# A decoder trunk in float32 on one core: the MLP's first matrices as token-major column pairs with 7-product steps, and the residual kept in HBM

## The chip, the cores and the metric

The kernel runs on one core of one Trainium2 chip. A core has five engines with queues of their own: PE (TensorE, the matrix multiplier, whose weight loads the profile lists apart as PEld), DVE (VectorE), ACT (ScalarE), POOL (GpSimd) and SP (SyncE, which here only issues DMA transfers). PE writes its results into PSUM, eight banks of 128 x 512 float32. Everything else works in SBUF, and the weights come from HBM. The metric is the time of one execution on the device in microseconds (us); the time before is the median of three runs.

## The reference, cut to what matters

A residual stream x of 256 tokens by 2048 goes through two layers. The first is a retention layer, the second a multi-head latent attention layer, and each is followed by an MLP with 8192 hidden columns:

```python
def rms_norm(x, gain):
    xf = x.astype(jnp.float32)
    y = xf * lax.rsqrt(jnp.mean(xf * xf, axis=-1, keepdims=True) + RMS_EPS)
    return (y * gain.astype(jnp.float32)).astype(x.dtype)

def sq_relu_mlp(h, w1, w2):
    return jnp.square(jax.nn.relu(h @ w1)) @ w2

for layer in range(DEPTH):              # DEPTH = 2
    if layer < N_A_LAYERS:              # layer 0
        x = x + retention(rms_norm(x, norm_mix[layer]), ...)
    else:                               # layer 1
        ...                             # shared keys and values from x
        x = x + mla_attention(rms_norm(x, norm_mix[layer]), ...)
    x = x + sq_relu_mlp(rms_norm(x, norm_mlp[layer]), mlp_w1[layer], mlp_w2[layer])
```

`mlp_w1[layer]` is 2048 x 8192 and `mlp_w2[layer]` is 8192 x 2048, all in float32.

## The kernel before

**Products.** A float32 product is made of three products of a faster type: each operand is split into a high part (a rounded copy, made by ACT) and a low part (the rest, made by DVE), and PE adds high x high, high x low and low x high. `split` (lines 139 to 148) makes the two parts, of weights as of activations. So every weight that streams in costs one ACT cast and one DVE subtraction, in pieces of 128 x 1024, into the buffers `wh` and `wl` (five of each). The raw weights come in chunks of 1 MB into three `raw` buffers, one SP transfer each.

**Activations.** An `act` tile (line 73, 20 buffers) holds the two parts of 256 feature rows for all 256 tokens, feature-major, that is, with features on partitions. Other scratch tiles of 2 KB per partition come from `f2k` (14 buffers). The residual x stays in SBUF for the whole kernel as eight tiles of 128 tokens x 512 columns (line 111). PSUM has four `acc` banks, two `tp` banks and a pair of banks `at`.

**The MLP** (`mlp`, from line 650) goes through the hidden columns in four groups of 2048. In each group it first makes the hidden columns (up), then multiplies them by their rows of the second matrix (down).

- Up, in this kernel, is `gemm_t` (line 212): eight column tiles of 256 hidden columns, each over 16 feature tiles of 128 rows. The weights are the stationary operand, so the result comes out feature-major. The high weights multiply both parts of the activations in one matmul of 512 columns (line 231), the low weights only the high part, 256 columns (line 227). `up` (from line 656) adds the two halves of each bank, multiplies by the token's norm (a row over tokens, `row`, made by `token_row`, lines 393 to 405), applies ReLU and squares, and splits the result into a `hid` tile.
- Down is `gemm_pair` (line 288): two pairs of column blocks (1024 output columns each), each over eight row pairs of 256 hidden rows. Here the activations are stationary and the weights stream, so the result is token-major. One row pair is `quad` (line 239): a 2 x 2 block product (two token blocks, two row blocks, two column blocks). Five of the eight row pairs take the usual eight block products, 24 matmuls of 512 columns. The three row pairs named in `SEVEN` (line 32) take seven products instead, 21 matmuls, in the manner of Strassen and Winograd; for these, `quad` makes sums of the weight blocks on DVE (`u`, lines 270 to 276) and `up` makes sums of the activations' blocks (`hids`, lines 667 to 674). The accumulators c11, c12, c21 and c22 take the four `acc` banks, p1 and p5 the two `tp` banks, p6 and p7 the two banks of `at`.
- `pair_to_x` (line 322) ends a pair: twelve DVE additions from PSUM and SBUF into x, and two ACT copies.
- In the last group the second pair is computed as two plain blocks (`mlp_w2t`), so that the end of the layer isn't held up.

At a layer's border `into_next` (line 407) adds the block to x, sums its squares, and transposes the block on PE into `act` tiles for the next layer (`x_block_t`, line 365), scaled by the norm's gain. The norm of a token, a scalar, is applied afterwards.

**Order.** Work off the main line is put on a queue (`later`, line 81) that counts weight chunks: `later(2, turn)` emits `turn` two chunks later, and `need` runs the queue early when a step needs its results. That gives an order of urgency, not the order on the engines. A planner then places the instructions of each engine by its own costs, buffers and this urgency, and adds the semaphores; so on an engine an instruction written later can stand ahead of one written earlier. Once placed, each engine runs its instructions in that order.

In the attention, `score` makes the softmax of two heads on DVE and ACT, and its `turn` (lines 913 to 924) transposes the probabilities on PE (tile `ptp`), `later(2, ...)` after the scores.

Of the kernel before, what the change touches and what calls it, by code (L numbers as in the profile page):

```python
# [11 lines left out]
F32 = mybir.dt.float32  # L12
# [19 lines left out]
SEVEN = (1, 4, 7)  # L32
# [18 lines left out]
def yoco(ctx: ExitStack, tc: tile.TileContext, a):  # L51
# [59 lines left out]
    x = [[pool.tile([P, 512], F32, name=f"x_{t}_{b}") for b in range(NB)] for t in range(NT)]  # L111
# [176 lines left out]
    def gemm_pair(w, chunk0, act, kinds, name, done):  # L288
# [33 lines left out]
    def pair_to_x(c, b):  # L322

        for (t, j), key in (((0, 0), "c11"), ((0, 1), "c12"), ((1, 0), "c21"), ((1, 1), "c22")):
            nc.vector.tensor_tensor(x[t][b + j], c[key], x[t][b + j], op=ALU.add)
        p1, p5, v, u = (f2k([512], f"pair_{i}") for i in range(4))
        nc.scalar.copy(p1, c["p1"])
        nc.scalar.copy(p5, c["p5"])
        nc.vector.tensor_tensor(v, c["p6"], p1, op=ALU.add)
        nc.vector.tensor_tensor(u, c["p7"], v, op=ALU.add)  # L330
        nc.vector.tensor_tensor(x[0][b], x[0][b], p1, op=ALU.add)
        nc.vector.tensor_tensor(v, p5, v, op=ALU.subtract)
        nc.vector.tensor_tensor(p5, p5, u, op=ALU.subtract)
        nc.vector.tensor_tensor(x[0][b + 1], x[0][b + 1], v, op=ALU.add)
        nc.vector.tensor_tensor(x[1][b], x[1][b], u, op=ALU.add)
        nc.vector.tensor_tensor(x[1][b + 1], x[1][b + 1], p5, op=ALU.add)
# [28 lines left out]
    def x_block_t(b, g0s, outs, name):  # L365

        for k2 in range(2):
            tp = transposed(
                lambda t, j: x[t][b][:, (2 * k2 + j) * P : (2 * k2 + j + 1) * P], f"{name}_tp{b}{k2}"
            )  # L370
            for g0, out in zip(g0s, outs):
                v = act_tile(f"{name}{g0}_{b}{k2}")
                split_act(v, tp, [gain(g0 + b * 4 + k2 * 2 + j) for j in range(2)])
                out.append(v)
# [9 lines left out]
    def add_to_x(acc, b, ss, name):  # L384
        for t in range(NT):
            if acc is not None:
                nc.vector.tensor_tensor(x[t][b], acc[t], x[t][b], op=ALU.add)
            if ss is not None:
                square_sum(x[t][b], ss[t][:, b : b + 1], f"{name}_{t}{b}")

    row = pool.tile([P, S], F32, name="row")

    def token_row(r, row, name):

        wide = f2k([NT, P], f"{name}_wide")
        for t in range(NT):
            nc.vector.tensor_copy(wide[:, t], r[t].to_broadcast([P, P]))

        def turn():
            tp = bank("tp", [S], f"{name}_rtp")  # L400
            for t in range(NT):
                nc.tensor.transpose(tp[:, t * P : (t + 1) * P], wide[:, t], ident)
            nc.scalar.copy(row, tp)

        later(1, turn)

    def into_next(ss, g0s, outs, r, name, row=None):


        def done(b, acc):  # L410
            add_to_x(acc, b, ss, name)
            later(1, lambda: x_block_t(b, g0s, outs, name))
            if b == NB - 1:
                r.extend(x_rstd(ss, name))
                if row is not None:
                    token_row(r, row, name)

        return done
# [95 lines left out]

    def load_x(b):
        for t in range(NT):
            nc.sync.dma_start(x[t][b], a["x"][t * P : (t + 1) * P, b * 512 : (b + 1) * 512])
            square_sum(x[t][b], ss0[t][:, b : b + 1], f"n0_{t}{b}")
# [85 lines left out]
    for h in range(RH):  # L604
# [39 lines left out]
    act, r = [], []  # L644
    gemm_blocks(
        a["ret_w_out"], lambda b: b * 8, y_act, 32, "ro", into_next(ss, [G_MLP0], [act], r, "n1", row)
# [3 lines left out]
    def mlp(layer, act, row, done):  # L650
        w1, w2 = a[f"mlp_w1_{layer}"], a[f"mlp_w2_{layer}"]
        f0 = 0
        for gi, nf in enumerate(GROUPS):
            hid = []

            def up(acc, f):
                u = f2k([2, S], f"u{layer}_{f}")
                for i in range(2):
                    nc.scalar.copy(u[:, i], acc[i][:, S:])
                    nc.vector.tensor_tensor(u[:, i], acc[i][:, 0:S], u[:, i], op=ALU.add)  # L660
                both = row.unsqueeze(1).to_broadcast([P, 2, S])
                nc.vector.scalar_tensor_tensor(u, u, 0.0, both, op0=ALU.max, op1=ALU.mult)
                nc.scalar.activation(u, u, AF.Square)
                v = act_tile(f"hid{layer}_{f}")
                split_act(v, u)
                more = None
                if f - 2 * f0 in SEVEN:
                    blocks = u.rearrange("p j (t n) -> p (j t) n", t=NT)
                    sums = f2k([4, P], f"us{layer}_{f}")
                    nc.vector.tensor_tensor(sums[:, 0:2], blocks[:, 0:2], blocks[:, 1:4:2], op=ALU.subtract)  # L670
                    nc.vector.tensor_tensor(sums[:, 2], sums[:, 1], blocks[:, 0], op=ALU.subtract)
                    nc.vector.tensor_tensor(sums[:, 3], blocks[:, 2], sums[:, 2], op=ALU.add)
                    more = act_tile(f"hids{layer}_{f}")
                    split_act(more, sums.rearrange("p (j t) n -> p j (t n)", j=2))
                hid.append(v)
                both_hid.append((v, more))

            both_hid = []
            for f in range(2 * f0, 2 * (f0 + nf)):
                gemm_t(w1, f * 2, act, KD, f"u{layer}_{f}", lambda acc, f=f, f0=f0: up(acc, f))  # L680
            last = gi == len(GROUPS) - 1
            for p in range(2):
                if last and p:
                    for b in (2, 3):
                        gemm(
# [11 lines left out]
                gemm_pair(  # L697
                    w2, p * 32 + 2 * f0, both_hid, [i in SEVEN for i in range(2 * nf)], f"d{layer}_{gi}{p}", add
                )
# [4 lines left out]
    mlp(0, act, row, into_next(ss, [G_KV, G_MIX1], [act_kv, act_q], r2, "n2"))  # L704
# [170 lines left out]
    def score(b, qt, qpe):  # L875
# [48 lines left out]
        later(2, turn)  # L924
# [15 lines left out]
    gemm_blocks(a["mla_w_o"], lambda b: b * 4, o_act, KD, "wo", into_next(ss, [G_MLP1], [act], r, "n3", row))  # L940

    def finish(b, acc):
        if acc is not None:
            add_to_x(acc, b, None, "")
# [3 lines left out]
    mlp(1, act, row, finish)  # L948
# [90 lines left out]
```

## Time and profile before

| | |
|---|---|
| median of three runs | 2540.93 us (2538.68 to 2542.39) |
| the profiled execution's own time | 2538.38 us |
| its span, first to last instruction | 2536.5 us |
| mean granted TensorE clock | 1.000 |
| HBM read / written | 469.70 MB / 2.10 MB |
| POOL busy | 103.4 us |

The profile records every instruction with engine, start and duration. A group row names the line, the engine, the operation, the tile written, the tiles read, shapes and count; then come total busy time, mean duration in ns, and the engine's idle time just before these instructions with what ended it. In the timeline, rows give the start and the time from the first start to the last end of the instructions merged in the row. PE's matmuls are pipelined, so the records of neighbours overlap and what one costs is the distance between starts, not the duration.

### The profile page before, as it was taken

What the parts mean: (1) busy time and instruction counts of PE and PEld (TensorE: products, weight loads), DVE (VectorE), ACT (ScalarE), POOL (GpSimd) and SP (SyncE); (2) the same over time, 40 slices, a digit from 0 to 9 for tenths busy, and PEclk for the clock granted to TensorE, in tenths of its full rate; (3) what the DMA queues carried; (4) which work ended last, traced back from release to release, by engine and by line L of the source; (5) the groups of instructions that cost most, each with busy time, mean ns of one, the idle gap of its engine ahead of it and who ended that gap; (6) DMA issues with size and microseconds to landing.
All of it is one profiled execution on the core that took longest, in us unless ns stands there. A gap on an engine that the chain in (4) does not pass through costs nothing.

```text
span 2536.5 us, 32194 instructions
## 1 busy us (share of the span) xinstructions
PE 2516.8 (99%) x12710; PEld 2143.9 (85%) x12710; DVE 1758.4 (69%) x2336; ACT 1329.4 (52%) x1799; POOL 103.4 (4%) x131
## 2 busy tenths in 40 slices
PE   8999999999999999999999999999999999999999
PEld 7888888888888888888888888988888888888887
DVE  6655555554556786877877757877567868878775
ACT  6444444444445555555555656555555555555553
POOL 6200000000000000000000001100000000000000
PEclk9999999999999999999999999999999999999999
DMA  8555555545555465555555464433554554545544
GB/s 297 180 182 184 181 180 177 187 183 183 189 192 183 171 227 183 189 209 184 198 198 193 149 216 170 160 131 138 180 186 183 205 193 170 219 176 205 198 178 166
DMA packets 71575, 473.88 MB, mean 187 GB/s; under 512 B 8192, under 2 KB 9344, under 8 KB 18176
## 3 DMA queue, kind: packets, MB, share of 16 engines
q1 hardware_dynamic: 71280, 471.78, 51.2%
q8 instruction: 100, 1.64, 0.3%
q14 instruction: 51, 0.42, 0.0%
q10 hardware_dynamic: 144, 0.05, 0.0%
HBM read 469.70 MB, written 2.10 MB: 186 GB/s over the span
## 4 chain that ended last, share of the span: by engine, by line
PE 94%; DVE 2%; POOL 2%; DMA 0%; ACT 0%; issue 0%; SPq 0%; DVEq 0%; ACTq 0%; POOLq 0%
PE u_acc L231 19%; PE u_acc L227 10%; PE d_c L312 6%; PE d_c L313 6%; PE d_c L311 6%; PE ro_acc L205 2%; PE ro_acc L204 2%; PE ro_acc L203 2%; PE rv_acc L205 2%; PE rv_acc L203 2%; PE rv_acc L204 2%; PE rk_acc L231 2%; PE rq_acc L231 2%; PE rg_acc L205 2%; PE rg_acc L204 2%; PE rg_acc L203 2%
## 5 line engine op out<-in xcount | busy, mean ns | idle before, releaser
L231 PE MATMUL u_acc<-n,u_wh 128*128 128x512 f32 x2048 | 718.4, 398 | 0.0
L227 PE MATMUL u_acc<-n,u_wl 128*128 128x256 f32 x2048 | 564.8, 281 | 0.0
L231 PEld LDWEIGHTS u_acc<-n,u_wh 128*128 128x128 f32 x2048 | 381.1, 188 | 88.9
L143 DVE TENSOR_TENSOR u_wl<-u_raw,u_wh 128x1024 fp32r<-128x1024 f32 x256 | 311.4, 1222 | 155.2 <-ACT u_wh L142 154.2
L227 PEld LDWEIGHTS u_acc<-n,u_wl 128*128 128x128 f32 x2048 | 386.6, 189 | 5.6
L142 ACT CAST u_wh<-u_raw 128x1024 fp32r<-128x1024 f32 x256 | 267.9, 1051 | 201.5 <-PE u_acc L231 151.5
L142 ACT CAST d_wh<-d_raw 128x1024 fp32r<-128x1024 f32 (+1 forms) x256 | 247.0, 983 | 160.4 <-PE d_c L313 82.3
L143 DVE TENSOR_TENSOR d_wl<-d_raw,d_wh 128x1024 fp32r<-128x1024 f32 (+1 forms) x256 | 280.4, 1130 | 33.4 <-ACT d_wh L142 32.8
L312 PE MATMUL d_c<-d_wl,hid 128*128 128x512 f32 x644 | 251.3, 390 | 0.0
L313 PE MATMUL d_c<-d_wh,hid 128*128 128x512 f32 x644 | 250.6, 389 | 0.0
L311 PE MATMUL d_c<-d_wh,hid 128*128 128x512 f32 x644 | 246.7, 389 | 0.0
L143 DVE TENSOR_TENSOR d_wl<-d_u,d_wh 128x1024 fp32r<-128x1024 f32 x84 | 101.7, 1222 | 79.9 <-ACT d_wh L142 79.9
L142 ACT CAST d_wh<-d_u 128x1024 fp32r<-128x1024 f32 x84 | 87.6, 1049 | 122.8 <-PE d_c L313 108.2
L312 PEld LDWEIGHTS d_c<-d_wl,hid 128*128 128x128 f32 x644 | 120.8, 188 | 28.2 <-DVE d_wl L143 2.7
L311 PEld LDWEIGHTS d_c<-d_wh,hid 128*128 128x128 f32 x644 | 120.9, 188 | 24.8
L313 PEld LDWEIGHTS d_c<-d_wh,hid 128*128 128x128 f32 x644 | 120.9, 188 | 24.4
L143 DVE TENSOR_TENSOR ro_wl<-ro_raw,ro_wh 128x1024 fp32r<-128x1024 f32 x64 | 78.4, 1225 | 84.2 <-ACT ro_wh L142 84.2
L143 DVE TENSOR_TENSOR rg_wl<-rg_raw,rg_wh 128x1024 fp32r<-128x1024 f32 (+1 forms) x68 | 79.5, 1174 | 60.8 <-ACT rg_wh L142 60.8
L142 ACT CAST ro_wh<-ro_raw 128x1024 fp32r<-128x1024 f32 x64 | 67.4, 1053 | 94.5 <-PE ro_acc L205 86.5
L143 DVE TENSOR_TENSOR rv_wl<-rv_raw,rv_wh 128x1024 fp32r<-128x1024 f32 x64 | 79.2, 1248 | 41.4 <-ACT rv_wh L142 41.4
L203 PE MATMUL rg_acc<-rg_wh,a 128*128 128x512 f32 x256 | 101.2, 396 | 5.3 <-ACT a L145 5.3
L142 ACT CAST rg_wh<-rg_raw 128x1024 fp32r<-128x1024 f32 (+1 forms) x68 | 67.8, 998 | 72.4 <-PE rv_acc L205 46.7
(313 smaller groups left out, 5135.4 us busy)
## 6 DMA issues: line engine op xcount, KB each, us to landing
u_raw<-in_mlp_w SPq DMA_DIRECT2D x128, 1024.0 KB, 4.8
d_raw<-in_mlp_w SPq DMA_DIRECT2D x112, 1024.0 KB, 4.8
rv_raw<-in_ret_w_gv SPq DMA_DIRECT2D x32, 1024.0 KB, 4.8
ro_raw<-in_ret_w_out SPq DMA_DIRECT2D x32, 1024.0 KB, 4.8
rg_raw<-in_ret_w_gv SPq DMA_DIRECT2D x28, 1024.0 KB, 4.7
uq_raw<-in_mla_w_uq SPq DMA_DIRECT2D x24, 768.0 KB, 4.2
rq_raw<-in_ret_w_qk SPq DMA_DIRECT2D x16, 1024.0 KB, 4.8
rk_raw<-in_ret_w_qk SPq DMA_DIRECT2D x16, 1024.0 KB, 4.8
```

What stands on the lines that cost most here:

```text
L142: nc.scalar.copy(h, src)
L143: nc.vector.tensor_tensor(l, src, h.bitcast(F32), op=ALU.subtract)
L203: nc.tensor.matmul(acc[t], ah, rh, start=k == 0, stop=False)
L204: nc.tensor.matmul(acc[t], ah, rl, start=False, stop=False)
L205: nc.tensor.matmul(acc[t], al, rh, start=False, stop=k == nk - 1)
L227: nc.tensor.matmul(acc[f][:, 0:S], wl[:, cols], a[:, 0], start=False, stop=False)
L231: nc.tensor.matmul(acc[f], wh[:, cols], a.rearrange("p i s -> p (i s)"), start=k == 0, stop=k == nk - 1)
L311: nc.tensor.matmul(dst, ah, bh, start=n == 0, stop=False)
L312: nc.tensor.matmul(dst, ah, bl, start=False, stop=False)
L313: nc.tensor.matmul(dst, al, bh, start=False, stop=n == total[key] - 1)
```

## The change

Four things change together.

1. The first matrices of the MLP are stored in the same blocks as the second ones (`_quads`), and up uses `gemm_pair`: eight pairs of column blocks of 1024 hidden columns per layer, two per group, each over eight row pairs of 256 features. Three of the eight row pairs take seven products. So the layer's input, too, gets sums of its blocks for these row pairs (`with_sums`, called from `x_block_t`). The result is token-major: the token's norm is applied as a scale of ACT's Relu, and four hidden tiles per pair are transposed on PE, squared by ACT and split, with sums where needed. The token row goes.
2. The 7-product row pairs are numbers 3, 5 and 7 instead of 1, 4 and 7.
3. A pair ends in `pair_out`: six ACT copies out of PSUM, then eight DVE instructions, into `f2k` tiles. For up they are the hidden columns. For down they are added to the residual in HBM by accumulating DMA transfers that POOL issues, except in the last group of a layer, where they are added to x in SBUF. The residual lives in HBM (`x_home`) and is loaded into `act` tiles (`x_tiles`) before the retention's output matrix, before the last group's down matrices of each layer, and before the attention's output matrix; at each layer border it is stored again. The first load of x, for its squares, goes to scratch tiles. There are 24 `act` buffers instead of 20.
4. In the attention the transposes of the probabilities come `later(3)` instead of `later(2)`.

```diff
-SEVEN = (1, 4, 7)
+SEVEN = (3, 5, 7)
...
-        return pool.tile([P, 2, 2, S], dtype, tag="act", bufs=20, name=name)
+        return pool.tile([P, 2, 2, S], dtype, tag="act", bufs=24, name=name)
...
-    x = [[pool.tile([P, 512], F32, name=f"x_{t}_{b}") for b in range(NB)] for t in range(NT)]
+    dram = ctx.enter_context(tc.tile_pool(name="dr", bufs=1, space=bass.MemoryType.DRAM))
+    x_home = [[dram.tile([P, 512], F32, name=f"xh_{t}_{b}") for b in range(NB)] for t in range(NT)]
+    x = [[None] * NB for t in range(NT)]
+
+    def x_tiles(home, name):
+
+        for b in range(NB):
+            both = act_tile(f"x_{name}{b}", F32)
+            for t in range(NT):
+                x[t][b] = both[:, t].rearrange("p i s -> p (i s)")
+                nc.gpsimd.dma_start(x[t][b], home(t, b))
...
-                queue.append((clock[0] + 1, -1, lambda: done(made)))
+                queue.append((clock[0] + 1, -1, lambda: done(pair_out(made, name))))
...
+    def pair_out(c, name):
+
+        o = {}
+        for key in ("c22", "c12", "c11", "c21", "p1", "p5"):
+            o[key] = f2k([512], f"{name}_{key}")
+            nc.scalar.copy(o[key], c[key])
+        v, u = (f2k([512], f"{name}_{i}") for i in "vu")
+        nc.vector.tensor_tensor(v, c["p6"], o["p1"], op=ALU.add)
         nc.vector.tensor_tensor(u, c["p7"], v, op=ALU.add)
...
+        nc.vector.tensor_tensor(v, o["p5"], v, op=ALU.subtract)
+        nc.vector.tensor_tensor(o["p5"], o["p5"], u, op=ALU.subtract)
+        for key, add in (("c11", o["p1"]), ("c12", v), ("c21", u), ("c22", o["p5"])):
+            nc.vector.tensor_tensor(o[key], o[key], add, op=ALU.add)
+        return [[o["c11"], o["c12"]], [o["c21"], o["c22"]]]
+
+    def with_sums(blocks, name):
+
+        blocks = blocks.rearrange("p j (t n) -> p (j t) n", t=NT)
+        sums = f2k([4, P], f"{name}_sum")
+        nc.vector.tensor_tensor(sums[:, 0:2], blocks[:, 0:2], blocks[:, 1:4:2], op=ALU.subtract)
+        nc.vector.tensor_tensor(sums[:, 2], sums[:, 1], blocks[:, 0], op=ALU.subtract)
+        nc.vector.tensor_tensor(sums[:, 3], blocks[:, 2], sums[:, 2], op=ALU.add)
+        more = act_tile(f"{name}_more")
+        split_act(more, sums.rearrange("p (j t) n -> p j (t n)", j=2))
+        return more
...
+                elif 2 * b + k2 in SEVEN:
+                    u = f2k([2, S], f"{name}u_{b}{k2}")
+                    for j in range(2):
+                        nc.scalar.activation(u[:, j], tp[:, j], AF.Copy, scale=scales[j])
+                    split_act(v, u)
+                    out.append((v, with_sums(u, f"{name}{b}{k2}")))
...
             add_to_x(acc, b, ss, name)
-            later(1, lambda: x_block_t(b, g0s, outs, name))
+            blocks = [x[t][b] for t in range(NT)]
+            for t in range(NT):
+                nc.gpsimd.dma_start(x_home[t][b], blocks[t])
+            later(1, lambda: x_block_t(blocks, b, g0s, outs, name, sums))
...
+            def up(c, p, hid=hid, blocks=blocks):
+
+                need(r, NT)
+                for t in range(NT):
+                    for i in range(2):
+                        nc.scalar.activation(c[t][i], c[t][i], AF.Relu, scale=r[t])
+
+                def turn():
+                    for q in range(4):
+                        name = f"hid{layer}_{p}{q}"
+                        tp = transposed(
+                            lambda t, j: c[t][q // 2][:, (q % 2 * 2 + j) * P : (q % 2 * 2 + j + 1) * P], f"{name}_tp"
+                        )
+                        u = f2k([2, S], f"{name}_u")
+                        nc.scalar.activation(u, tp, AF.Square)
+                        v = act_tile(name)
+                        split_act(v, u)
+                        blocks.append((v, with_sums(u, name) if len(blocks) in SEVEN else None))
+                        hid.append(v)
+
+                later(1, turn)
+
+            for p in range(f0 // 2, (f0 + nf) // 2):
+                gemm_pair(
+                    w1, p * 8, act, [i in SEVEN for i in range(8)], f"u{layer}_{p}", lambda c, p=p, up=up: up(c, p)
+                )
+            if last:
+                x_tiles(lambda t, b: x_home[t][b], f"mlp{layer}")
...
-                    pair_to_x(c, 2 * p)
-                    if last:
-                        done(2 * p, None)
-                        done(2 * p + 1, None)
...
+                    for j in range(2):
+                        b = 2 * p + j
+                        if last:
+                            done(b, [c[t][j] for t in range(NT)])
+                            continue
+                        for t in range(NT):
+                            nc.gpsimd.dma_start(x_home[t][b], c[t][j], accum_op=ALU.add)
...
-        later(2, turn)
+        later(3, turn)
...
-        arrays[f"mlp_w1_{i}"] = _chunks(g["mlp_w1"][i], 256, 8)
+        arrays[f"mlp_w1_{i}"] = _quads(g["mlp_w1"][i])
```

More of the change, by code (lines that the diff above doesn't have):

```diff
@@ L653, in mlp @@
         for gi, nf in enumerate(GROUPS):
[L654 to L676, printed above, removed]
@@ L678, in mlp @@
-            both_hid = []
-            for f in range(2 * f0, 2 * (f0 + nf)):
-                gemm_t(w1, f * 2, act, KD, f"u{layer}_{f}", lambda acc, f=f, f0=f0: up(acc, f))
-            last = gi == len(GROUPS) - 1
+            hid, blocks = [], []
+            kinds = [i in SEVEN for i in range(2 * nf)]
+            last = gi == len(GROUPS) - 1
+            def up(c, p, hid=hid, blocks=blocks):
[16 more added lines that the diff above has]
+                later(1, turn)
@@ L684, in mlp @@
                     for b in (2, 3):
+                        need(hid, 2 * nf)
                         gemm(
```

70 lines of the change are left out of this document (25 added, 45 removed).

## The prediction

> **What bounds the kernel now.** I read the page first: the engines' busy time, then the chain that ended last, then the groups of instructions. From the page:
>
> ```profile
> span 2536.5 us, 32194 instructions
> PE 2516.8 (99%) x12710; PEld 2143.9 (85%) x12710; DVE 1758.4 (69%) x2336; ACT 1329.4 (52%) x1799; POOL 103.4 (4%) x131
> PE 94%; DVE 2%; POOL 2%; DMA 0%; ACT 0%; issue 0%; SPq 0%; DVEq 0%; ACTq 0%; POOLq 0%
> ```
>
> PE is busy nearly all the time and carries 94% of the chain, so a change is worth what it takes off PE's stream, less any new wait of PE. The view by windows, cut where the MLP of layer 0 passes from its first matrix (up) to its second (down) and back, gives the prices. The columns are the stretch, its length, then busy us of PE, PEld, DVE, ACT, POOL, the granted clock, the DMA share and GB/s:
>
> ```profile
> 750.40:841.70 91.30, 91.30 (x524) 79.40 (x523) 61.16 (x81) 50.17 (x72) 1.52 (x4) 1.00 0.51 185
> 841.70:924.90 83.20, 83.20 (x368) 68.53 (x367) 70.49 (x81) 46.91 (x53) 0.00 (x0) 1.00 0.50 189
> 924.90:1015.10 90.20, 90.20 (x514) 78.37 (x512) 65.33 (x82) 47.19 (x64) 0.00 (x0) 1.00 0.55 199
> 1015.10:1098.20 83.10, 83.10 (x367) 68.48 (x366) 70.39 (x81) 46.88 (x53) 0.00 (x0) 1.00 0.50 189
> ```
>
> PE has no gap in any of them and the granted clock is 1.00. An up stage of 8 column tiles takes 90.2 us (512 matmuls); a down stage of two column pairs takes 83.1 us (366 matmuls: per pair five row pairs of 24 and three of 21). The first stage is 1.1 us longer, since the transposes of the layer's input lie in it. DVE is the second busiest, 70.4 of 83.1 us in a down stage.
>
> **The up matrices as column pairs.** In the new kernel two up pairs replace one up stage. A column pair of the first matrix has 8 row pairs (2048 rows), three of them with 7 products: 183 matmuls of 128x512, just as a down pair. So I take the down stage's row for two of them: 83.1 us instead of 90.2, 7.1 us less in each of 8 stages (4 groups, 2 layers): **-57 us**. The down stages keep their count, since SEVEN still holds 3 of 8.
>
> **The transposes.** The output now lies token-major, so each up pair turns 4 hidden tiles with 4 transposes each: 16 x 16 = 256. A row of before's transposes (starts, durations):
>
> ```profile
> L162 PE MATMUL n_tp<-cst,x 128*128 128x128 f32 x96 | 12.6, 272 | 0.0
> 756.01 1.04 PE L162 MATMUL n_tp<-cst,x 128*128 128x128 f32 x8
> 756.80 0.36 PE L227 MATMUL u_acc<-n,u_wl 128*128 128x256 f32 x1
> 757.00 0.40 PE L231 MATMUL u_acc<-n,u_wh 128*128 128x512 f32 x1
> 757.24 0.28 PE L227 MATMUL u_acc<-n,u_wl 128*128 128x256 f32 x1
> 757.36 0.39 PE L231 MATMUL u_acc<-n,u_wh 128*128 128x512 f32 x1
> ```
>
> Each record lasts 272 ns, but they overlap: eight start at 756.01, and the matmul after the next starts at 757.00, where it normally follows its forerunner by 0.12 us (757.24 to 757.36). Eight therefore cost 757.00 - 0.12 - 756.01 = 0.87 us, 0.11 each: 256 x 0.11 = **+28 us**. [...]
>
> **DVE and ACT in an up pair.** Durations:
>
> ```profile
> L143 DVE TENSOR_TENSOR d_wl<-d_raw,d_wh 128x1024 fp32r<-128x1024 f32 x214 | 251.5, 1217 | 21.3 <-ACT d_wh L142 20.6
> L271 DVE TENSOR_TENSOR d_u<-d_raw 128x1024 f32<-128x1024 f32 x42 | 51.2, 1218 | 0.2
> L275 DVE TENSOR_TENSOR d_u<-d_u,d_raw 128x512 f32<-128x512 f32 x42 | 28.7, 684 | 0.3
> L143 DVE TENSOR_TENSOR hid<-u,hid 128x512 fp32r<-128x512 f32 x64 | 44.0, 687 | 5.7 <-ACT hid L142 5.7
> L670 DVE TENSOR_TENSOR us<-u 128x256 f32<-128x256 f32 x24 | 10.0, 417 | 0.0
> L672 DVE TENSOR_TENSOR us<-u,us 128x128 f32<-128x128 f32 x24 | 6.8, 283 | 0.0
> L663 ACT ACTIVATE u<-u 128x512 f32<-128x512 f32 x64 | 40.6, 634 | 14.5 <-DVE u L662 14.4
> L142 ACT CAST d_wh<-d_raw 128x1024 fp32r<-128x1024 f32 x214 | 221.9, 1053 | 109.6 <-PE d_c L313 45.7 <-PE u_acc L231 16.6 <-PE d_acc L205 14.3
> L328 ACT COPY pair<-d_p 128x512 f32<-128x512 f32 x14 | 8.1, 580 | 0.3
> 892.98 5.76 DVE L143 TENSOR_TENSOR d_wl<-d_raw,d_wh 128x1024 fp32r<-128x1024 f32 x5
> 887.10 0.68 DVE L332 TENSOR_TENSOR pair<-pair,pair 128x512 f32<-128x512 f32 x1
> 887.70 0.68 DVE L335 TENSOR_TENSOR x<-x,pair 128x512 f32<-128x512 f32 x1
> ```
>
> Back to back a 1024-wide DVE instruction advances (5.76 - 1.22) / 4 = 1.135 us and a 512-wide one 0.60 us (887.10 to 887.70). An up pair needs on DVE: splits of 1024, 5 x 2 + 3 x 3 = 19, and 3 sums d_u, 22 x 1.135 = 25.0; 512-wide 3 splits, 6 sums, 8 of pair_out, 4 hidden splits, 21 x 0.60 = 12.6; the sums of 1.5 hidden tiles about 1.5 x (0.42 + 2 x 0.28 + 0.60) = 2.4. Together 40.0 us under PE's 41.6 + 1.8 = 43.4 us: 92%. What went: the adds, the product with the token row and the split of each up tile. A down pair of before asks 22 x 1.135 + 21 x 0.60 = 37.6 of 41.6 us (90%; some of it is done in the up stage behind, so the window shows 85%) and PE didn't wait; in the new kernel it loses 4 of the adds (the residual goes by DMA), 35.2 us. ACT, at recorded durations: 19 x 1.05 + 3 x 0.62 + 6 copies x 0.58 + 4 Relu, 4 Square, 4 splits x 0.63 + 1.5 x 0.62 = 33.8 us, 78%. So both hide behind PE, DVE barely: I take **0** for throughput, and the bound upwards is a rival.
>
> **The turn at a pair's end.** After an up pair's last product DVE adds, ACT applies Relu, and one tick later PE transposes, ACT squares, DVE splits. PE runs in order, so it waits wherever the planner put a transpose ahead of late data. Rows that price it, from the waits and from a down-to-down border of before:
>
> ```profile
> PE ptp L918 <- DVE p L911: 6.4, 4, 2.1
> PE ptp L918 <- ACT wo_wh L142: 1.7, 1, 1.7
> ACT u_wh L142 <- DMA u_raw<-in_mlp_w: 23.2, 12, 2.9
> ...
> 882.50 1.22 DVE L143 TENSOR_TENSOR d_wl<-d_raw,d_wh 128x1024 fp32r<-128x1024 f32 x1
> 883.63 0.68 DVE L329 TENSOR_TENSOR pair<-d_p,pair 128x512 f32<-128x512 f32 x1
> 884.23 1.21 DVE L143 TENSOR_TENSOR d_wl<-d_raw,d_wh 128x1024 fp32r<-128x1024 f32 x1
> 885.36 0.68 DVE L330 TENSOR_TENSOR pair<-d_p,pair 128x512 f32<-128x512 f32 x1
> ...
> 882.90 0.39 PE L313 MATMUL d_p<-d_wh,hids 128*128 128x512 f32 x1
> 883.12 0.84 PE L311 MATMUL d_c<-d_wh,hid 128*128 128x512 f32 x3
> ```
>
> At the border the planner laces the next chunk's splits between the four adds, and PE goes on at 883.12, 0.22 us after the last product, with the products that need only the high part. So the four accumulator banks can change hands without a gap. The two `tp` banks hold p1 and p5 of the 7-product row pairs and are also what the transposes need; the first of these row pairs is now number 3, so `tp` is free for three row pairs, 16 us, before p1 claims it: 0. With 16 up pairs the turn lies between 0 (n_tp: PE idle 0.0) and 16 x 2.1 = 34 us (ptp, a chain of softmax that was late each time). Its chain is u, two differences, four adds and a Relu, some 7 x 0.6 + 0.6 = 4.8 us, and a row pair of 24 matmuls (24 x 0.227 = 5.4 us) is queued ahead of it, so it is nearest to n_tp: I take 0.4 each, **+6 us**.
>
> **The residual.** It leaves SBUF: 24 tiles of 256 KB are stored (8 at each of three layer borders), 12 down pairs (3 groups x 2 x 2 layers) add 4 tiles each by DMA, and 8 tiles are read four times, all from POOL's queue, which before held only the tables and the norms' small steps. No accumulating DMA is in the trace. Nearest rows:
>
> ```profile
> d_raw<-in_mlp_w SPq DMA_DIRECT2D x112, 1024.0 KB, 4.8
> x<-in_x SPq DMA_DIRECT2D x8, 256.0 KB, 9.1
> out<-x SPq DMA_DIRECT2D x8, 256.0 KB, 2.6
> ```
>
> One tile lands in 2.6 to 9.1 us. The sources are held until then, 4 of 14 `f2k` buffers, and the next burst is 41 us away; the sums are read back a whole up stage later. What can hurt is the weight stream: its 16 engines are half busy (0.50 to 0.55 above), and a burst adds 1 MB to be read and written. If it delays a chunk as the longest DMA wait of ACT did (2.9 us) and PE felt it, 12 x 2.9 = 35 us; below, 0, for in before PE waited for none of those 12, so it is nearest to 0: I take 0.2 a burst, **+2 us**. A gain is excluded, as no transfer disappears. The reads wait for a free `act` slot (24, were 20) and stand ahead of the norms' power on POOL; that result is wanted at the first pair's end, 41 us later: 0.
>
> **The softmax one tick later.** `later(2)` becomes `later(3)`; a tick is a chunk of 24 matmuls of 384 columns, 24 x 0.227 x 0.75 = 4.1 us, the wait at most 2.1. Of the two ptp rows the 6.4 us go, and I keep the 1.7, since the turn now falls on the tick of the next query's work: **-6 us** (ends: 0 and -8.1). The token row's four transposes also go: -0.4. The sums of the layer input's three tiles are new, 3 x 1.6 us of DVE per layer, wanted 16 us or more later: 0.
>
> **Sum**, against the profiled execution's 2538.4 us (span 2536.5 plus 1.9): 2538.4 - 57 + 28 + 6 + 2 - 6 - 0.4 = 2511. That execution lies 2.5 us below the median of the runs, 2540.9, within their spread; I forecast **2511 us**, 1.2% less. Differences up to 0.2%, 5 us, are about what a measurement of this kernel can't tell from no change.
>
> **Rivals.**
> A. DVE becomes the bound. If what counts is not the spacing but the recorded duration, an up pair costs 22 x 1.22 + 21 x 0.69 + 2.5 = 43.8 us, and with waits for ACT's casts of 1 us some 45: as much as half an up stage now. Then the whole gain of the first matrices is gone and 2538 - 6 = 2532 remains. For it: 92% is more than any stage of before held for long, and it is asked without pause, up and down alternating. Against: the five splits in 5.76 us, and the down stage at 90% without a gap.
> B. On the other side: the end-of-pair chain stands ahead of the next pair's first splits, on DVE and ACT in order. PE then stops for 4.8 us of chain and 1.2 us of the next split, 6 us at each of 16 up pairs: 2511 - 6 + 96 = 2601. It decides from (2546 - 2505) / 16 = 2.6 us a pair. Against: the laced rows at 882.50 to 885.36. For: there ACT had two copies in the chain; now it has six copies and four Relu, and the Relu wait for DVE's adds.
> C. Transposes cost their record. With 272 ns apiece 256 make 70 us and the sum is 2553. Against: eight starting within 0.8 us. [...]
> D. The DMA bursts starve the weights, 35 instead of 2 us: 2544, about no change. For: read, add and write share the 16 engines. Against: they are half idle.
>
> **Chances.** Forecast, 2497 to 2522: 0.46. A and partial stalls, 2522 to 2536: 0.22. Better, as less is lost at the turns and both ptp rows go, below 2497: 0.03. No change within 5 us, D mostly: 0.06. Slower: 0.23 (B 0.17, C 0.03, D worse 0.03). That gives faster 0.71, same 0.06, slower 0.23. The range 2494 to 2558 leaves out the deep part of B and little else; the likeliest case's own range is 2497 to 2522.
>
> **What would show it.** By windows: an up stage of two pairs near 87 us with PE busy throughout, and down stages still 83.1 (57 and 28 right). DVE near 80 us in an up stage. Hidden tiles' transposes with idle time near 0 before them on PE; some 2 us before each would be the turn's upper end, 6 us on DVE's weight splits B. The wait of ptp gone from PE's list. The accumulating transfers landing in under 41 us, with PE waits on no DMA. The prediction is wrong if PE's gaps in the MLP add up to more than 30 us, or if its matmuls no longer start 0.227 us apart there.

## The result and the profile after

The changed kernel takes 2535.9 us in the median (2529.5 to 2541.9) beside 2540.1 us for the kernel before on the same chips: a ratio of 0.9982, with a 95% interval of 0.9975 to 0.9989. That is 4 us of gain where 29 were forecast. The profiled execution took 2535.5 us.

From the page of the changed kernel, the lines that answer to those shown of before (span, busy time by engine, share of the chain that ended last):

```profile
span 2533.7 us, 31133 instructions
PE 2504.2 (99%) x11794; PEld 2092.5 (83%) x11794; DVE 1912.6 (75%) x2478; ACT 1442.1 (57%) x1993; POOL 180.2 (7%) x235
PE 73%; DVE 16%; ACT 5%; issue 2%; POOL 2%; DMA 2%; SPq 0%; ACTq 0%; DVEq 0%; POOLq 0%
```

PE lost 12.6 us of busy time (2516.8 to 2504.2), but it now carries 73% of the chain and no longer 94%; DVE went from 2% to 16%. The view by windows of the changed kernel (stretch, length, busy us of PE, PEld, DVE, ACT and POOL, granted clock, DMA share, GB/s) shows the first four stages of layer 0's MLP, up and down in turn, and the last down stage of layer 1:

```profile
754.90:840.70 85.80, 85.80 (x391) 71.08 (x390) 73.29 (x87) 55.81 (x76) 4.84 (x6) 1.00 0.55 190
840.70:927.50 86.80, 86.02 (x383) 69.68 (x382) 77.33 (x92) 54.16 (x72) 3.58 (x4) 1.00 0.63 206
927.50:1012.40 84.90, 84.90 (x383) 70.27 (x382) 75.58 (x86) 53.40 (x69) 3.48 (x4) 1.00 0.63 211
1012.40:1099.20 86.80, 86.00 (x383) 69.70 (x382) 77.27 (x91) 54.09 (x72) 3.48 (x4) 1.00 0.62 206
2435.90:2533.70 97.80, 90.16 (x392) 72.51 (x391) 67.76 (x82) 45.72 (x58) 0.00 (x0) 0.97 0.46 161
```

An up stage is 84.9 us (90.2 before), and PE is busy in all of it. A down stage is 86.8 (83.1 before), with a gap of 0.8 us in PE. The last one has 7.6 us of gaps, and its mean granted clock is 0.97.

The same boundaries, taken through both traces, account for the whole difference of the spans:

| stretch | before, us | after, us | difference |
|---|---|---|---|
| up to the retention's output matrix | 570.7 | 575.2 | +4.5 |
| eight up stages | 724.3 | 682.2 | -42.1 |
| six middle down stages | 499.0 | 521.2 | +22.2 |
| last down stage of layer 0 | 87.8 | 93.9 | +6.1 |
| last down stage of layer 1, to the end | 89.3 | 97.8 | +8.5 |
| attention: query and output matrices | 243.4 | 241.3 | -2.1 |
| everything else | 322.1 | 322.1 | 0 |

What PE waited for in the changed kernel (engine, tile and line that waited, releaser; us in total, times, longest):

```profile
PE d_acc L214 <- DVE d_wl L153: 4.5, 3, 2.9
PE ao L955 <- ACT pt L946: 4.2, 3, 2.9
PE d_c L322 <- DVE d_wl L153: 4.2, 7, 0.7
PE tr_tp L172 <- DVE tr_scaled L510: 3.9, 2, 3.3
```

These are the rows that the change brought or made longer; the longest single wait, 5.8 us of `rg_acc` in the first 6 us of the kernel, was there before with 5.3. Before, `tr_tp` cost 1.1 us, `ptp` 8.1, and the other three rows weren't there. Two of the four are waits for DVE's weight splits in down stages: `d_c` at a change of pairs, `d_acc` in the plain blocks that end a layer. The timeline of DVE in the changed kernel shows one, at the change from the first pair of the down stage at 1012.4 to the second. PE starts the second pair near 1056.6:

```profile
1055.12 1.23 DVE L153 TENSOR_TENSOR d_wl<-d_raw,d_wh 128x1024 fp32r<-128x1024 f32 x1
1056.58 0.69 DVE L344 TENSOR_TENSOR d_c<-d_c,d_p 128x512 f32<-128x512 f32 x1 [0.23 <-ACT d_p L337]
1057.19 0.69 DVE L339 TENSOR_TENSOR d_v<-d_p,d_p 128x512 f32<-128x512 f32 x1
1057.91 0.69 DVE L340 TENSOR_TENSOR d_u<-d_p,d_v 128x512 f32<-128x512 f32 x1
1058.52 1.22 DVE L153 TENSOR_TENSOR d_wl<-d_raw,d_wh 128x1024 fp32r<-128x1024 f32 x1
1059.65 0.68 DVE L341 TENSOR_TENSOR d_v<-d_p,d_v 128x512 f32<-128x512 f32 x1
...
1062.06 0.69 DVE L344 TENSOR_TENSOR d_c<-d_c,d_p 128x512 f32<-128x512 f32 x1
1062.66 4.63 DVE L153 TENSOR_TENSOR d_wl<-d_raw,d_wh 128x1024 fp32r<-128x1024 f32 x4
```

and PE's timeline beside it:

```profile
1062.19 1.07 PE L321 MATMUL d_c<-d_wh,hid 128*128 128x512 f32 x4
1063.93 0.50 PE L322 MATMUL d_c<-d_wl,hid 128*128 128x512 f32 x1 [0.67 <-DVE d_wl L153]
```

DVE makes the two splits of the second pair's first row pair (1055.12, 1058.52), and laces the eight additions of `pair_out` around the later one. The splits of the second row pair come after the last addition, at 1062.66. PE takes the four products that need only the high part at 1062.19 and then waits until 1063.93. Its starts lie 1.06 us apart instead of 0.23 there. This comes back at all six middle changes (1.04 to 1.07 us each).

### The profile page after: what moved, and what is told of

It is laid out like the page before. It is cut to its first block, busy times and chain, and to the rows that moved or that the text cites. A ratio compares the mean times of both kernels' runs of the same rounds, so it can differ in the third digit from the quotient of the medians.

```text
span 2533.7 us, 31133 instructions
## 1 busy us (share of the span) xinstructions
PE 2504.2 (99%) x11794; PEld 2092.5 (83%) x11794; DVE 1912.6 (75%) x2478; ACT 1442.1 (57%) x1993; POOL 180.2 (7%) x235
## 4 chain that ended last, share of the span: by engine, by line
PE 73%; DVE 16%; ACT 5%; issue 2%; POOL 2%; DMA 2%; SPq 0%; ACTq 0%; DVEq 0%; POOLq 0%
DVE d_wl L153 7%; PE u_c L322 6%; PE u_c L323 6%; PE u_c L321 6%; PE ro_acc L215 2%; PE ro_acc L214 2%; PE ro_acc L213 2%; PE rv_acc L215 2%; PE rv_acc L213 2%; PE rv_acc L214 2%; ACT d_wh L152 2%; PE rk_acc L241 2%; PE rq_acc L241 2%; PE d_c L322 2%; PE rg_acc L215 2%
## 5 line engine op out<-in xcount | busy, mean ns | idle before, releaser
L153 DVE TENSOR_TENSOR u_wl<-u_raw,u_wh 128x1024 fp32r<-128x1024 f32 (+1 forms) x256 | 278.7, 1118 | 25.7 <-ACT u_wh L152 25.1
L322 PE MATMUL u_c<-u_wl,n 128*128 128x512 f32 x736 | 287.6, 391 | 0.3 <-DVE u_wl L153 0.2
L321 PE MATMUL u_c<-u_wh,n 128*128 128x512 f32 x736 | 287.4, 390 | 0.0
L323 PE MATMUL u_c<-u_wh,n 128*128 128x512 f32 x736 | 286.4, 389 | 0.0
L152 ACT CAST d_wh<-d_raw 128x1024 fp32r<-128x1024 f32 (+1 forms) x256 | 239.5, 988 | 61.2 <-DMA d_raw<-in_mlp_w 29.9
L152 ACT CAST u_wh<-u_raw 128x1024 fp32r<-128x1024 f32 (+1 forms) x256 | 238.2, 978 | 60.5 <-PE u_c L323 37.0
L152 ACT CAST u_wh<-u_u 128x1024 fp32r<-128x1024 f32 x96 | 96.6, 1048 | 180.3 <-DVE u_u L286 164.4
L322 PEld LDWEIGHTS u_c<-u_wl,n 128*128 128x128 f32 x736 | 138.2, 188 | 29.5 <-DVE u_wl L153 1.6
L321 PEld LDWEIGHTS u_c<-u_wh,n 128*128 128x128 f32 x736 | 138.2, 188 | 28.5
L323 PEld LDWEIGHTS u_c<-u_wh,n 128*128 128x128 f32 x736 | 138.2, 188 | 28.4
L153 DVE TENSOR_TENSOR u_wl<-u_u,u_wh 128x1024 fp32r<-128x1024 f32 x96 | 113.9, 1222 | 55.0 <-ACT u_wh L152 55.0
```

Source lines behind the costliest of these rows:

```text
L152: nc.scalar.copy(h, src)
L153: nc.vector.tensor_tensor(l, src, h.bitcast(F32), op=ALU.subtract)
L321: nc.tensor.matmul(dst, ah, bh, start=n == 0, stop=False)
L322: nc.tensor.matmul(dst, ah, bl, start=False, stop=False)
L323: nc.tensor.matmul(dst, al, bh, start=False, stop=n == total[key] - 1)
```

## The experiments

Theory: in a down pair DVE is late with the next weights, because the pair ends with a 7-product row pair and the additions of `pair_out` follow at once. A 7-product row pair asks DVE for some 6.3 us (four instructions of 1.135 and three of 0.60, by the prediction's spacing), and PE for 21 x 0.227 = 4.8; a usual one asks for 2.3 and 5.4. Rivals: the accumulating transfers hold something up; the changed placements elsewhere cost it; or DVE's total work is simply too much.

All ratios are to the kernel before on the same chip, with their 95% interval; the changed kernel's own is 0.9982. An edit is made to the changed kernel unless another is named.

**e1: no accumulating transfers.**

```diff
-                        for t in range(NT):
-                            nc.gpsimd.dma_start(x_home[t][b], c[t][j], accum_op=ALU.add)
```

> The accumulating transfers of the six middle groups are left out (the output lacks what those groups' down matrices add), everything else stands. Theory DVE (the eight or twelve additions at a down pair's end stand ahead of the next splits on DVE, and PE waits for the low parts): the middle down stages stay at 86.8 us and the time stays within 5 us of the changed kernel's 2536. Theory DMA (the bursts delay the weight chunks; ACT waited 29.9 us for d_raw): the middle down stages fall by some 1.5 to 2 us each to about 85, the time by 9 to 12 us.

2532.8 us, 0.9969 (0.9957 to 0.9981). The view of waits:

```profile
PE d_acc L214 <- DVE d_wl L153: 4.7, 3, 2.9
PE d_c L322 <- DVE d_wl L153: 4.1, 6, 0.7
```

The output lacks what these transfers add. The waits and the down stages of 86.8 us stay as they were, though ACT's waits for the landing of `d_raw` fall from 29.9 to 17.1 us. So the transfers don't cause PE's waits, and are worth at most about 3 us.

**e2: the last four additions of a down pair on POOL.**

```diff
+    def pair_out(c, name, last_adds):
...
-            nc.vector.tensor_tensor(o[key], o[key], add, op=ALU.add)
+            last_adds.tensor_tensor(o[key], o[key], add, op=ALU.add)
```

Down pairs pass POOL as `last_adds`, up pairs DVE.

> The last four additions of a down pair go from DVE to POOL, 4 x 0.6 = 2.4 us less on DVE behind the border; POOL needs some 1.5 to 2.4 us for each, and nothing waits for them but the transfers. Theory DVE: the waits at the border (0.8 us in six middle stages, 2 to 5 us in the two last ones with the slow matmuls that follow) mostly go, 6 x 0.8 + 5 = about 10 us less than the changed kernel. Theory DMA: no change within 3 us.

2562.1 us, 1.0083 (1.0069 to 1.0097): 26 us slower than the changed kernel, where 10 us of gain were expected. The groups show why; the second row is the same instruction in an up pair of the same run, where POOL adds nothing:

```profile
L341 DVE TENSOR_TENSOR d_v<-d_p,d_v 128x512 f32<-128x512 f32 x14 | 25.1, 1790 | 0.0
L341 DVE TENSOR_TENSOR u_v<-u_p,u_v 128x512 f32<-128x512 f32 x16 | 11.0, 685 | 0.0
L344 POOL TENSOR_TENSOR d_c<-d_c,d_v 128x512 f32<-128x512 f32 x14 | 26.3, 1879 | 1.4 <-DVE d_v L341 1.4
```

The additions that left take 1879 ns on POOL, and one that stayed on DVE takes 1790 instead of 685 (last section). PE's waits on `d_wl` rose:

```profile
PE d_c L322 <- DVE d_wl L153: 11.1, 6, 3.2
PE d_acc L214 <- DVE d_wl L153: 7.6, 4, 3.8
```

Waits on `u_wl` in up pairs, 0.2 us in the changed kernel, rose to 12.0 us, too. So the run doesn't tell what fewer additions are worth (e7 does), but more time on DVE at this place means longer waits of PE.

**e3: the 7-product row pairs moved off the end of the pair.** Every engine has the same instructions, in another order.

```diff
-SEVEN = (3, 5, 7)
+SEVEN = (2, 4, 6)
```

> The 7-product row pairs become numbers 2, 4 and 6, so a pair ends with a plain row pair, in which DVE needs 2.3 us of PE's 5.4. Theory DVE: DVE comes to the border 3 us less behind, and the waits there go: 6 x 0.8 + 5 = about 10 us less than the changed kernel. Theory DMA: no change. In both p1 claims its bank one row pair earlier; if the transposes of the turn aren't through by then, 16 turns lose up to 1 us each.

2519.5 us, 0.9917 (0.9904 to 0.9931), 16 us below the changed kernel; 10 were expected. PE's waits in the MLP are now

```profile
PE hid_tp L172 <- ACT u_c L683: 3.7, 4, 1.6
```

and no row names `d_wl`. The middle down stages take 85.3 to 86.1 us, the two last 92.3 and 91.8. In DVE's timeline the splits run ahead before the additions come:

```profile
1048.93 7.04 DVE L153 TENSOR_TENSOR d_wl<-d_raw,d_wh 128x1024 fp32r<-128x1024 f32 x6
1056.14 1.23 DVE L281 TENSOR_TENSOR d_u<-d_raw 128x1024 f32<-128x1024 f32 x1 [0.17 <-DMA d_raw<-in_mlp_w]
1057.40 0.69 DVE L285 TENSOR_TENSOR d_u<-d_u,d_raw 128x512 f32<-128x512 f32 x1
1058.01 0.68 DVE L339 TENSOR_TENSOR d_v<-d_p,d_p 128x512 f32<-128x512 f32 x1
```

Three windows hold the first pair of the down stage near 1010 us: the changed kernel, e3, and e11 (below).

```profile
1012.40:1056.60 44.20, 44.08 (x200) 35.56 (x199) 40.04 (x52) 29.99 (x43) 0.00 (x0) 1.00 0.55 191
```

```profile
1011.60:1056.30 44.70, 43.91 (x201) 35.68 (x200) 41.27 (x52) 30.88 (x43) 0.00 (x0) 1.00 0.52 189
```

DVE has 40.0 us of work in the one and 41.3 in the other, with the wait after the first and without it after the second. So it isn't the amount of DVE's work alone but where it stands.

**e7: the last four additions of each down pair left out.**

```diff
         for key, add in (("c11", o["p1"]), ...):
+            if name[0] == "d":
+                break
             nc.vector.tensor_tensor(o[key], o[key], add, op=ALU.add)
```

> The changed kernel with the last four additions of each down pair left out (the output lacks those terms), nothing put in their place. Theory DVE: PE's wait at the border of the two down pairs (1.06 us from start to start) goes in the six middle groups, and the waits of the two last groups shrink: 8 to 12 us less than the changed kernel. If instead it is the copies on ACT or the landing of the weights, the waits stay and the time is the same within 3 us. Against the run with these additions on POOL it tells whether POOL itself was what cost 26 us.

2524.6 us, 0.9936 (0.9924 to 0.9949). The output lacks these terms. With the order (3, 5, 7) kept, one wait on `d_wl` in middle down pairs is left, of 0.5 us, and the middle down stages fall from 86.8 to 85.8 (one to 86.6), the last ones to 90.7 and 92.9. The additions are needed for the wait, too.

**e11: the residual in HBM and the new end of a pair, but the first matrices as before** (feature-major, with the token row).

```diff
-            for p in range(f0 // 2, (f0 + nf) // 2):
-                gemm_pair(
-                    w1, p * 8, act, [i in SEVEN for i in range(8)], f"u{layer}_{p}", lambda c, p=p, up=up: up(c, p)
-                )
+            for f in range(2 * f0, 2 * (f0 + nf)):
+                gemm_t(w1, f * 2, act, KD, f"u{layer}_{f}", lambda acc, f=f, up=up: up(acc, f))
```

> The changed kernel with the first matrices as before (column tiles of 256, feature-major, no turn), so only the residual in HBM, the new end of a pair, the row pairs 3, 5, 7 and later(3) are left. Theory DVE in the form that the new end of a pair is enough (its additions in one block behind ACT's copies): the border of the two down pairs shows PE's wait of about 1 us in the middle groups and the last two stages their 3 to 5 us, and with later(3) and the late first load the time is some 2536 to 2542. If it needs the up pairs' load too (DVE at 65 instead of 80 us in an up stage, no turn in the down stage), the borders have no wait and the time is about 2535 plus 3 for the first load, 2536 to 2538, with down stages of 83.1 us.

2539.9 us, 0.9996 (0.9988 to 1.0005): no change. Its middle down stages take 83.0 us and have no wait at the border, with the order (3, 5, 7) and the same eight additions. The window of its first pair:

```profile
1018.30:1059.80 41.50, 41.50 (x185) 34.34 (x183) 32.73 (x38) 24.56 (x31) 0.00 (x0) 1.00 0.47 177
```

Here DVE has 32.7 us of work where the changed kernel has 40.0, since no up pair's end and hidden tiles fall into it. So the wait needs three things: the heavy row pair last, the additions behind it, and a DVE that has had no slack before. Its up stages are 90.3 us.

**e4: the first load of x into `act` tiles** and not into the `f2k` scratch.

```diff
+        both = act_tile(f"x0_{b}", F32)
...
-            x0 = f2k([512], f"x0_{t}{b}")
+            x0 = both[:, t].rearrange("p i s -> p (i s)")
```

> The first load of x goes to act tiles instead of f2k tiles. If the loads were late because they waited for f2k buffers that POOL's tables held (SP waited 7.7 us for tr_part), the gap of PE before the table's transposes at 58 us falls from 3.7 to 0.8 us, as before the change, and 3 to 4 us go with the slow matmuls behind it. If the square sums or POOL's norm are late for another reason, the gap stays.

2532.7 us, 0.9967 (0.9956 to 0.9979). The retention's output matrix starts at 571.5 us and not at 575.2, and the row `tr_tp` is gone. In the changed kernel SP's list has the cause, a load of x waiting for scratch that POOL still held:

```profile
SPq L536 <- POOL tr_part L459: 7.7, 1, 7.7
```

**e5 and e6: the softmax's turn.** e5 puts the changed kernel back to two ticks, e6 gives the kernel before three and changes nothing else.

```diff
-        later(3, turn)
+        later(2, turn)
```

> The changed kernel with the transposes of the probabilities two chunks after the scores again, as before. By the windows the attention's last two stages went from 243.4 to 241.3 us, so I expect 2 us more than the changed kernel, with the five waits of 1.6 to 2.2 us before ptp back and the waits before ao (1.4 and 3.3 us) gone. If later(3) is worth the 6 us that the prediction took, it is 6 us more.

> The kernel before with later(3) alone. Expected 2 us less than before (0.9992) if new waits before ao take the place of those before ptp whatever the rest; 6 to 8 us less (0.997) if these new waits come from the other parts of the change.

e5: 2537.6 us, 0.9990 (0.9981 to 0.9999). e6: 2535.0 us, 0.9979 (0.9970 to 0.9988), on its own as much as the whole change. The waits of `ptp` (1.8 to 2.1 us between starts) come back in e5 and go in e6, where

```profile
PE ao L929 <- ACT pt L920: 4.5, 3, 2.9
```

takes their place: the product with the values, one tick after the turn, is now the late one.

**e8, e9, e10, e12: what is the change worth without these losses?** e9 is e3 with the load of e4 and the values' product at `later(2)`. e10 is e9 with the hidden tiles' turn at `later(2)`. e8 is e10 with SEVEN = (3, 5, 6). e12 gives the kernel before what e10 has of general use: SEVEN = (2, 4, 6), and the softmax's turn and values' product as in e10. The edits of e10, without the load of e4 shown above:

```diff
-SEVEN = (3, 5, 7)
+SEVEN = (2, 4, 6)
...
-                later(1, turn)
+                later(2, turn)
...
-            later(1, lambda: values(b, pt))
+            later(2, lambda: values(b, pt))
```

> A version: 7-product row pairs 3, 5 and 6 (a pair ends with a plain row pair, and the tp banks stay free for three), the turn two row pairs after the pair's end instead of one, x's first load in act tiles, the values one chunk later. Theory DVE with the turn's wait (1 to 2 us before hid_tp in four groups of the run with 2, 4, 6): middle down stages at 85.0, the last two at 90 and 88, the start 3 us shorter: some 2508 us by the clock of the run with 2, 4, 6 (2519). If two adjoining 7-product row pairs (DVE 6.4 of PE's 4.8 us each) are worse for DVE than the end of the pair, new waits appear inside the pairs and it is not faster than 2519.

> A version: 7-product row pairs 2, 4 and 6, x's first load in act tiles, the values (tile ao) one chunk later. Each part was worth on its own: 16 us (the order), 3 us (the first load), and some 3 us for the waits before ao (1.4 and 3.3 us), which the run with 3, 5 and 6 no longer had. If they add up, 6 us less than the 2519 of the run with 2, 4, 6: 2513.

> The same with the turn two row pairs after the pair's end. If PE's waits of 1 to 2 us before hid_tp come from the turn being too close to the Relu, they go and the time is 3 to 5 us below the version without it. If the tp banks decide (p1 claims one at row pair 2, just when the turn wants both), new waits before u_p or d_p appear and it is the same or slower.

> The kernel before with the small edits of the fastest version that it can take: row pairs 2, 4 and 6, later(3) for the probabilities, the values one chunk later. If these edits are what makes that version fast, this one comes near its 2510 us. If the order of the row pairs only repairs waits that the up pairs brought (before had none at its borders), it gains later(3)'s 5 us and some 3 for the values, 2531 to 2535, and the remaining 20 to 25 us are the up pairs' own worth, close to the 29 that the prediction took for their matmuls less the transposes.

| | median, us | ratio (95%) | |
|---|---|---|---|
| e8 | 2519.6 | 0.9917 (0.9903 to 0.9930) | up stages 85.6 to 86.6, down 86.0 to 86.7 |
| e9 | 2512.8 | 0.9895 (0.9880 to 0.9910) | waits of `hid_tp`: 4.2 us |
| e10 | 2509.8 | 0.9883 (0.9870 to 0.9897) | none in middle stages |
| e12 | 2531.0 | 0.9961 (0.9947 to 0.9974) | up 90.3, down 83.0 |

e10 is the best version: 31 us below the kernel before and 26 below the changed one. An up and a down stage of e10:

```profile
922.60:1007.80 85.20, 85.09 (x383) 70.19 (x383) 75.62 (x87) 55.37 (x70) 3.49 (x4) 1.00 0.65 212
1007.80:1093.10 85.30, 85.18 (x384) 70.21 (x383) 76.72 (x91) 55.03 (x71) 3.49 (x4) 1.00 0.63 209
```

Against e12 its gain is 21 us: that is what the first matrices as pairs bring, together with the residual in HBM and the new end of a pair, where PE's waits in the middle stages are gone. e8 differs from e10 in SEVEN alone and is 10 us slower. It has no 7-product row pair at the end, but two of them in a row, and its waits lie inside the pairs:

```profile
PE u_c L322 <- DVE u_wl L153: 2.3, 9, 0.5
PE d_p L321 <- ACT d_wh L152: 1.7, 8, 0.2
```

These waits hold under half of the 10 us; where the rest lies wasn't traced. So it isn't the end alone: of the three orders that were run with up pairs, the one in which every 7-product row pair has a usual one behind it inside its own pair is the fastest.

## Why the prediction was wrong

The forecast was 2511 us, with 2497 to 2522 as its own range. The measured 2535.9 us lies in the case "No change within 5 us", which had a chance of 0.06 and for a reason, rival D, that the runs refute. Term by term, with what the runs showed:

| term | forecast | measured | from |
|---|---|---|---|
| up matrices as pairs | -57 | -57 | up stage 84.9 = 83.1 + 16 x 0.11; in e11 they are back at 90.3 |
| transposes | +28 | +28 | as above; the other half lies in the down stages |
| turn at a pair's end | +6 | about +7 | a remainder: what a down stage of e7 has over 83.1 + 1.8, 0.9 us in each of 8 |
| DVE and ACT, change of a pair | 0 | about +15 | 86.8 - 85.8 in six stages; about 3 and 6 in the last two |
| accumulating transfers | +2 | 0 to +3 | e1 |
| first load of x, no term | 0 | +4 | 4.5 later at the output matrix; e4 takes back 3.7 |
| softmax and token row | -6.4 | -2 | stage account; e5 (in the kernel before e6 shows -5) |

The measured column adds up to -5 to -2 us; the spans differ by -2.8.

**What was right.** The price of both layouts, taken from the down stage's row, and that of the transposes, taken from distances and not from records (the group of 256 is recorded at 281 ns each): rival C is refuted, since it would make an up stage 83.1 + 16 x 0.27 = 87.4 us. An up stage "near 87" beside down stages "still 83.1", as the prediction's signs had it, didn't come for a smaller reason: the second up pair's transposes, half of the 28 us, lie in the down stage. The accumulating transfers land in 7.0 us, far under 41, and no wait of PE names one: rival D falls.

```profile
L172 PE MATMUL hid_tp<-cst,u_c 128*128 128x128 f32 x256 | 36.6, 281 | 0.9
xh<-d_c POOLq DMA_DIRECT2D x48, 256.0 KB, 7.0
```

**The step that failed** is "So both hide behind PE, DVE barely: I take 0 for throughput", with its support "So the four accumulator banks can change hands without a gap". This term, taken as 0, measured about 15 us. Two things were wrong in it. The first was to compare DVE and PE by sums over a pair, 35 to 40 us against 42 to 43. Inside a pair the load is uneven, and with 7, the heaviest row pair, last and the additions behind it, DVE owes the most just where PE starts on new weights. The second was to read the change of pairs off the kernel before, where DVE came into it with more slack: e11 shows that this border does stay without a gap if the up matrices aren't pairs. The change itself added DVE work to the first down pair, the end of the up pair and its hidden tiles. The prediction counted that in an up pair and not in the down pair that it falls into.

Neither DVE rival was it. A made DVE too slow by total, and e3 has the same total without the waits. B had the mechanism, an end-of-pair chain ahead of the next splits, but put it at the 16 up pairs with 6 us each. It came at the down pairs, and cost about 1 us where eight additions stand between the splits, and more in the last down stages, where those of the residual in SBUF are mixed in.

The last down stage of layer 1 shows it at its worst. The timeline of DVE, the end of twelve additions and the splits behind them, in the changed kernel:

```profile
2486.67 1.88 DVE L417 TENSOR_TENSOR x_mlp<-d_c,x_mlp 128x512 f32<-128x512 f32 x3
2488.47 5.75 DVE L153 TENSOR_TENSOR d_wl<-d_raw,d_wh 128x1024 fp32r<-128x1024 f32 x5
```

PE waits for that split until 2489.74, and 0.9 us later its granted clock goes from 1.00 (2489.74 to 2490.60) to 0.50 (2490.70 to 2494.00; last section).

**The smaller misses.** "The sums of the layer input's three tiles ... 0" held. The first load of x had no term at all, though the change moves it to another kind of buffer; the trace of before showed that POOL works on the rotary tables then, and whose buffers they use could be read in the code. In the softmax the step "Of the two ptp rows the 6.4 us go" was right, but what is late next wasn't looked up: the values' product, one tick behind the turn.

**What stays open.** e7 and e3 put the border between 11 and 16 us, and don't add up exactly, since each moves some other waits (e7 has 1.6 us in up pairs, e3 3.7 at the hidden tiles). The accumulating transfers' 0 to 3 us aren't told apart from no cost.

## What to carry to other kernels

Where one engine feeds another through a few buffers, compare them not over a loop but from one handover to the next, and put the step that is heaviest for the feeder where a light one follows: the same instructions in another order were worth 16 us here, four times the gain of the change. A border without a gap in the old kernel is no evidence for the new one, if the change adds work to the engine that feeds it. And when a wait is removed by moving a step later, look for the consumer of that step: it inherits the wait unless it moves, too.

## What the runs showed of the hardware

**In e2 a DVE addition beside one on POOL took 2.6 times as long.** Additions with both inputs in SBUF went from 685 ns to 1790 on DVE (the rows above). The timelines of one pair's end show it. POOL first:

```profile
1060.01 1.29 POOL L344 TENSOR_TENSOR d_c<-d_c,d_p 128x512 f32<-128x512 f32 x1 [119.65 <-ACT d_p L337]
1062.21 1.83 POOL L344 TENSOR_TENSOR d_c<-d_c,d_u 128x512 f32<-128x512 f32 x1
1064.95 1.93 POOL L344 TENSOR_TENSOR d_c<-d_c,d_v 128x512 f32<-128x512 f32 x1
```

and DVE:

```profile
1061.67 1.22 DVE L153 TENSOR_TENSOR d_wl<-d_raw,d_wh 128x1024 fp32r<-128x1024 f32 x1
1062.80 1.79 DVE L341 TENSOR_TENSOR d_v<-d_p,d_v 128x512 f32<-128x512 f32 x1
1064.52 1.21 DVE L153 TENSOR_TENSOR d_wl<-d_raw,d_wh 128x1024 fp32r<-128x1024 f32 x1
1065.65 1.78 DVE L342 TENSOR_TENSOR d_p<-d_p,d_u 128x512 f32<-128x512 f32 x1
```

Beside POOL's first addition DVE runs L339 and L340, which read one input from PSUM; it takes 1.29 us, and they take 0.69, as in the changed kernel. The second starts during a split, and ends at 1064.04, 1.24 us after DVE went on to its next instruction. That one, L341, ends at 1064.59, 0.55 us after POOL's. The next two repeat it: POOL ends at 1066.88, 1.23 us after DVE went on from the split at 1065.65, and L342 at 1067.43, again 0.55 us later. Whether one of the two waits for the other, or both run slower side by side, the run doesn't show.

**In the 4 us after three waits of PE, of 2.0 to 2.9 us, its granted clock was 0.50 to 0.58; after two others, of 2.9 and 3.2 us, it was 1.00.** Windows of the changed kernel, of the 4 us after the wait of 2.9 us in the last down stage and of the 4 us after another of 2.9 us, ended at 1736.95:

```profile
2490.00:2494.00 4.00, 4.00 (x12) 3.10 (x12) 4.00 (x4) 0.57 (x2) 0.00 (x0) 0.58 0.59 194
1737.00:1741.00 4.00, 4.00 (x11) 3.24 (x12) 2.70 (x6) 1.43 (x2) 0.00 (x0) 0.50 0.27 41
```

The granted clock is 0.58 in the 4 us after the wait in the last down stage and 0.50 after the other. In the last down stage matmuls start 0.427 us apart there instead of 0.227: eight of them cost 1.6 us more, on top of the wait. After the same wait in e5, 2.9 us and ended at 2492.28, the clock is 1.00:

```profile
2492.30:2496.30 4.00, 4.00 (x17) 3.27 (x18) 4.00 (x4) 1.23 (x2) 0.00 (x0) 1.00 0.66 179
```

In e2 it is 1.00 after a wait of 3.2 us, ended at 2356.63, and 0.57 after one of 2.0 us, ended at 1259.17:

```profile
2356.60:2360.60 4.00, 3.97 (x17) 3.30 (x18) 3.45 (x4) 1.04 (x2) 0.00 (x0) 1.00 0.43 129
1259.20:1263.20 4.00, 4.00 (x11) 3.13 (x12) 3.41 (x5) 1.05 (x1) 0.00 (x0) 0.57 0.47 133
```

So in these five the clock doesn't follow the length of the wait. What decides it isn't shown: no run varies it on purpose.
